# Bounding the decays of a chunked scan on ScalarE, by a relu and an exponential with biases, in place of a subtract-and-min on VectorE

## The chip, the cores and the metric

The kernel runs on one core of a Trainium2 chip. The time of a kernel is the device time of one execution in microseconds (us); lower is better. A profiled execution also leaves a trace, whose span is a little shorter than the execution's time.

## What is computed

The reference is one layer of a hybrid block over 256 tokens with 256 context tokens: a projection, two mixers (S5, a diagonal state space model, and SSD, a chunked scan), a merge, and a mixture of 32 experts. The change lies in SSD, where every head needs, within each chunk of 128 positions, the matrix of decays from position s to position l, times the step dt of position s:

```
def decay_matrix(a_cum):
    ...
    diff = a_cum[..., :, None] - a_cum[..., None, :]
    return jnp.where(mask, jnp.exp(jnp.where(mask, diff, 0.0)), 0.0)
...
    a_cum = jnp.moveaxis(jnp.cumsum(dtc * a.reshape(SSD_GROUPS, SSD_HPG), axis=2), 2, -1)
    cb = jnp.einsum('bclgn,bcsgn->bcgls', cc, bc)
    lmat = decay_matrix(a_cum) * dt_t[..., None, :]
    y_diag = jnp.einsum('bcgls,bcgrls,bcsgrp->bclgrp', cb, lmat, x)
    y_off = jnp.einsum('bclgn,bcgrpn,bcgrl->bclgrp', cc, prev, jnp.exp(a_cum))
```

There are 8 groups of 4 heads, two directions, and two chunks of the 256 tokens: 8 x 2 = 16 sets of 4 x 2 = 8 blocks of 128 x 128.

## The kernel before, in words

The program has three parts in time: some 50 us of preparation, the mixers (50 to 690 us of the span), and then the merge, the router and the experts, which stream 402 MB of weights from memory.

The mixers are written as 14 streams (generators), among them `gemm` (the projection, in blocks of 4 x 128 rows), `conv`, `gates_z`, `prep`, `ssd`, `decays`, and the S5 streams `turned`, `vgen`, `states`, `tables` and `outputs`. A planner (class Plan) takes from them, step by step, the step that could start first by its own cost estimates, and writes the instructions in that order. Each engine (PE, DVE = VectorE, ACT = ScalarE, POOL, and SP, which only starts DMAs) then works through its own list in order. The planner calls all instructions through one helper, so that they all carry line 1442; they are told apart by their tiles.

For each block of `gemm`, SP loads 128 x 512 weights `w`, ACT rounds them to `h` (CAST h<-w), DVE or POOL subtracts to get the rest, again `h` (TENSOR_TENSOR h<-w,h), and PE multiplies both parts into a bank `mm`. At most LOOK = 2 blocks are cut ahead of the one that PE multiplies. Two `mm` banks alternate: a column's bank becomes free when `conv` has read it (one ACT and four DVE instructions for `cv`), when ACT has copied it out (`us`, `zt`), or, for the gate columns at the end, when ACT has taken the sigmoid.

Before the mixers `ssd_dt` makes the cumulative sums `a_cum`: as rows in memory (`acd`), and as columns `acs`, one number per partition, chunk and head. `lnd` is ln(dt), again as columns. Of `acs` ln(dt) is taken off at once (line 441).

`decays` makes set n = 2 g + d_: SP loads four rows of `acd`, each copied to all 128 partitions, as `rt` (one buffer); DVE makes `et` = min(rt - acs, lnd) in 8 instructions of 128 x 128, one for each head and chunk, since acs and lnd are per-partition scalars (lines 922 to 927); ACT takes the exponential of `et` in one instruction of 128 x 1024 and of `rt` in another; POOL multiplies `rt` by C. So et = exp(min(a_l - a_s + ln dt_s, ln dt_s)): where l comes before s the min bounds it, and the mask is multiplied in later. `ssd` then multiplies `et` by the masked C B products `xl` on DVE, and PE multiplies `et` and `rt` into the bank `yps`. When PE has read set n - 1 (mark "used"), `rt` is loaded for set n. The group's output goes on through DVE (`mb`), ACT (`zt`), PE (`aux`), ACT (`rs`) and DVE (`dg`, `ybT`).

Of the kernel before, what the change touches and what calls it, by code (L numbers as in the profile page):

```python
# [13 lines left out]
AF = mybir.ActivationFunctionType  # L14
ALU = mybir.AluOpType
# [4 lines left out]
P = 128  # L20
# [26 lines left out]
def bcast(ap, axis, n):  # L47
    a = ap.unsqueeze(axis)
    shape = list(a.shape)
    shape[axis] = n  # L50
    return a.to_broadcast(shape)


def build(tc, I, out):
    nc = tc.nc
    dve, act, pe, pool, sp = nc.vector, nc.scalar, nc.tensor, nc.gpsimd, nc.sync
# [44 lines left out]
    def aux_ps(name="aux"):  # L101
        return ps.tile([P, 512], F32, tag="aux", name=name, bufs=2)
# [243 lines left out]
    def mm3(out, a, b, first, last):  # L346

        pe.matmul(out, a[0], b[0], start=first, stop=False)
        pe.matmul(out, a[0], b[1], start=False, stop=False)  # L349
        pe.matmul(out, a[1], b[0], start=False, stop=last)  # L350
# [24 lines left out]
    def ux(n):  # L375
        return lambda k: (uh[k // 4][:, k % 4, 0:n], ul[k // 4][:, k % 4, 0:n])
# [8 lines left out]
    def ssd_dt():  # L385
        act.activation(arow, arow, AF.Exp)
        wdh = H.tile([P, KD, 64], F32R, tag="h", name="wdh")
        act.copy(wdh, wdt)
        wdl = H.tile([P, KD, 64], F32R, tag="h", name="wdl")
        dve.tensor_tensor(wdl, wdt, wdh.bitcast(F32), op=ALU.subtract)  # L390
        pd = aux_ps()
        for k in range(KD):
            mm3(pd[0:64], (wdh[:, k], wdl[:, k]), ux(512)(k), k == 0, k == KD - 1)
        dtr = F.tile([64, 512], F32, tag="Ut", name="dtr")
        act.copy(dtr, pd[0:64])
        pt = aux_ps()
        for t in range(4):
            pe.transpose(pt[:, t * 64:(t + 1) * 64], dtr[:, t * P:(t + 1) * P], ident[0:64, 0:64])
        n = [-1]
        dtt = F.tile([P, 4, 4, 64], F32, tag="et", name="dtt", bufs=2)  # L400
        dtt = [dtt[:, i] for i in range(4)] + [F.tile([P, 4, 64], F32, tag="xtok", name="dtq", bufs=BUFS["xtok"])]

        def tt():
            n[0] += 1
            return dtt[n[0]]

        x, e, s_, s2, q = tt(), tt(), tt(), tt(), tt()
        dve.tensor_tensor(x, pt[:, 0:256].rearrange("p (t c) -> p t c", t=4), bcast(dtb, 1, 4), op=ALU.add)
        act.activation(e, x, AF.Abs)
        act.activation(e, e, AF.Exp, scale=-1.0)  # L410

        dve.tensor_scalar(s_, e, 2.0, None, op0=ALU.add)
        dve.reciprocal(s_, s_)
        dve.tensor_mul(s_, s_, e)
        dve.tensor_mul(s2, s_, s_)
        dve.tensor_scalar(q, s2, 1.0 / 15, None, op0=ALU.mult)
        for c_ in (13, 11, 9, 7, 5, 3):
            dve.scalar_tensor_tensor(q, q, 1.0 / c_, s2, op0=ALU.add, op1=ALU.mult)
        dve.scalar_tensor_tensor(q, q, 1.0, s_, op0=ALU.add, op1=ALU.mult)
        dve.tensor_scalar(x, x, 0.0, None, op0=ALU.max)  # L420
        dt = F.tile([P, 4, 64], F32, tag="dg", name="dt")
        dve.scalar_tensor_tensor(dt, q, 2.0, x, op0=ALU.mult, op1=ALU.add)
        dtA = F.tile([P, 4, 64], F32, tag="Cn", name="dtA")
        dve.scalar_tensor_tensor(dtA, dt, -1.0, bcast(arow, 1, 4), op0=ALU.mult, op1=ALU.mult)

        pr = aux_ps()
        pc = aux_ps()
        for c_ in range(2):
            for d_, tr in ((0, triU), (1, triL)):
                cols = slice(32 * d_, 32 * d_ + 32)  # L430
                pe.matmul(pr[cols, c_ * P:(c_ + 1) * P], dtA[:, c_, cols], tr, start=True, stop=True)
                pe.matmul(pc[:, c_ * 64 + 32 * d_:c_ * 64 + 32 * d_ + 32], tr, dtA[:, c_, cols], start=True, stop=True)
        arows = F.tile([64, 256], F32, tag="us", name="arows")
        act.copy(arows, pr[0:64, 0:256])
        acd = dram.tile([64, 256], F32, name="acd")
        act.dma_start(acd, arows)

        lnd = F.tile([P, 2, 64], F32, name="lnd")
        act.activation(lnd, dt[:, 0:2], AF.Ln)
        acs = F.tile([P, 2, 64], F32, name="acs")  # L440
        dve.tensor_tensor(acs, pc[:, 0:128].rearrange("p (c h) -> p c h", c=2), lnd, op=ALU.subtract)

        pw = aux_ps()
        f_, b_ = slice(0, 32), slice(32, 64)
        terms = [
            [(triLs, 2, f_), (ones, 3, f_)], [(triLs, 3, f_)],
            [(triUs, 2, b_)], [(triUs, 3, b_), (ones, 2, b_)],
            [(triLs, 0, f_)], [(triUs, 1, b_)],
            [(ones, 0, f_)], [(ones, 1, b_)],
        ]  # L450
        for i, tl in enumerate(terms):
            for j, (m_, t_, cl) in enumerate(tl):
                pe.matmul(pw[:, 32 * i:32 * i + 32], m_, dtA[:, t_, cl], start=(j == 0), stop=(j == len(tl) - 1))
        wend = F.tile([P, 8, 32], F32, name="wend")
        act.activation(wend.rearrange("p a b -> p (a b)"), pw[:, 0:256], AF.Exp)
        for i, tk, cl in ((0, 2, f_), (1, 3, f_), (2, 2, b_), (3, 3, b_), (4, 0, f_), (5, 1, b_)):
            dve.tensor_mul(wend[:, i, :], wend[:, i, :], dt[:, tk, cl])
        dsm.update(lnd=lnd, acs=acs, wend=wend, acd=acd)
# [6 lines left out]
    def mixers():  # L465
        plan = Plan(nc)
        pe, dve, act, pool, sp = plan.pe, plan.dve, plan.act, plan.pool, plan.sp
        tile_, mark, slot = plan.tile, plan.mark, plan.slot
        EP, Bb, r8, root = s5["EP"], s5["Bb"], s5["r8"], s5["root"]
        lnd, wend, acs, acd = dsm["lnd"], dsm["wend"], dsm["acs"], dsm["acd"]  # L470
# [442 lines left out]
        def decays():  # L913

            for n in range(2 * NG):
                g, d_ = n // 2, n % 2
                plan.at("decay", n / (2 * NG))
                yield ("sp", slot("rt", 1)) + ((("used", n - 1),) if n else ())
                rt = tile_(F, [P, 4, 256], F32, "rt")
                sp.dma_start(rt, acd[32 * d_ + 4 * g:32 * d_ + 4 * g + 4, :].partition_broadcast(P))  # L920
                et = tile_(F, [P, 4, 256], F32, "et", 2)
                for h in range(4):
                    yield "dve", rt
                    for c_ in range(2):
                        hh = 32 * d_ + 4 * g + h
                        dve.tensor_scalar(et[:, h, c_ * P:(c_ + 1) * P], rt[:, h, c_ * P:(c_ + 1) * P],
                                          acs[:, c_, hh:hh + 1], lnd[:, c_, hh:hh + 1], op0=ALU.subtract, op1=ALU.min)
                yield "act", et, AF.Exp
                act.activation(et, et, AF.Exp)
                act.activation(rt, rt, AF.Exp)  # L930
                yield "pool", rt, ("cv", g, 3)
                pool.tensor_tensor(rt, rt, bcast(cv[g, 3][:, 0], 1, 4), op=ALU.mult)
                dec[n] = rt, et
                mark(("dec", n))
# [143 lines left out]
        plan.add(prep(), "prep")  # L1078
        plan.add(ssd(), "out")
        plan.add(decays(), "decay")  # L1080
        plan.add(turned(), "other")
        plan.add(vgen(), "vgen")
# [5 lines left out]
        return ys[0]  # L1088

    ssd_dt()  # L1090
    for q4 in range(4):
        s5_inputs(q4)
# [174 lines left out]
    for t in range(2):  # L1267
# [15 lines left out]
                                 op0=ALU.add, op1=ALU.mult))  # L1283
# [47 lines left out]
class Plan:  # L1331
# [23 lines left out]
    def slot(self, tag, bufs):  # L1355

        of = self.slots.get(tag, [])
        return self.used.get(of[-bufs], 0.0) if len(of) >= bufs else 0.0

    def mark(self, name):  # L1360
        self.ready[name] = self.last
# [585 lines left out]
```

## Time and profile before

| | |
|---|---|
| median of 3 runs | 1853.15 us (1849.97 to 1854.26) |
| the profiled execution | 1846.35 us, span 1844.2 us |
| mixers | about 50 to 690 us of the span |
| busy over the span | PE 86%, DVE 49%, ACT 27%, POOL 16% |

Busy time is the time in which an engine works on an instruction; a wait is the idle time before an instruction, put down to what ended it. All shares below are of one profiled execution. A row's mean can exceed its busy time over its count, where instructions of one kind overlap.

### The profile page before, as it was taken

What the parts mean: (1) busy time and instruction counts of PE and PEld (TensorE: products, weight loads), DVE (VectorE), ACT (ScalarE), POOL (GpSimd) and SP (SyncE); (2) the same over time, 40 slices, a digit from 0 to 9 for tenths busy, and PEclk for the clock granted to TensorE, in tenths of its full rate; (3) what the DMA queues carried; (4) which work ended last, traced back from release to release, by engine and by line L of the source; (5) the groups of instructions that cost most, each with busy time, mean ns of one, the idle gap of its engine ahead of it and who ended that gap; (6) DMA issues with size and microseconds to landing.
All of it is one profiled execution on the core that took longest, in us unless ns stands there. A gap on an engine that the chain in (4) does not pass through costs nothing. (4 is left out here: it accounts for less than half of the span.)

```text
span 1844.2 us, 27968 instructions
## 1 busy us (share of the span) xinstructions
PE 1589.1 (86%) x11118; PEld 935.1 (51%) x11118; DVE 904.5 (49%) x1671; ACT 506.8 (27%) x893; POOL 290.0 (16%) x297
## 2 busy tenths in 40 slices
PE   6798888976988799897998888898888889988987
PEld 3576666764766698783533232333333444333443
DVE  7668899888898546664222222242222223212233
ACT  5333453552435565342111111111111111111111
POOL 5133445435331330100000000000000000000000
PEclk8899898987997999998999999999999999988998
DMA  8677554444542357784999999999998999999984
GB/s 309 181 236 237 178 144 136 119 121 110 148 127 64 114 155 264 235 281 161 417 418 417 417 418 417 413 418 417 418 410 350 418 417 418 418 417 419 418 349 174
DMA packets 141415, 539.36 MB, mean 292 GB/s; under 512 B 31736, under 2 KB 44952, under 8 KB 91920
## 3 DMA queue, kind: packets, MB, share of 16 engines
q1 hardware_dynamic: 136032, 526.95, 75.7%
q10 hardware_dynamic: 4608, 7.95, 1.3%
q8 instruction: 143, 2.34, 0.5%
q0 software_dynamic: 560, 1.52, 0.3%
q14 instruction: 72, 0.59, 0.1%
HBM read 529.60 MB, written 6.77 MB: 291 GB/s over the span
## 5 line engine op out<-in xcount | busy, mean ns | idle before, releaser
L1519 PE MATMUL p_gu<-mw,xe 128*64 128x512 f32 x2048 | 474.8, 601 | 45.2 <-DMA mw<-in_mu 28.4
L1442 PE MATMUL mm<-uh,h 128*128 128x256 f32 (+1 forms) x1152 | 323.6, 361 | 45.2 <-DVE cv L1442 29.9
L1519 PEld LDWEIGHTS p_gu<-mw,xe 128*64 128x64 f32 x2048 | 174.2, 137 | 335.7 <-issue 176.8
L1442 PEld LDWEIGHTS mm<-uh,h 128*128 128x128 f32 x1152 | 209.6, 201 | 85.4 <-issue 42.3
L1629 PE MATMUL p_y<-mw,aT 128*64 128x512 f32 x1024 | 243.4, 627 | 3.4 <-issue 3.4
L1442 PE MATMUL mm<-ul,h 128*128 128x256 f32 (+1 forms) x576 | 202.5, 352 | 0.0
L1442 POOL TENSOR_TENSOR h<-w,h 128x512 fp32r<-128x512 f32 x99 | 150.3, 1522 | 279.3 <-ACT h L1442 213.6
L1637 DVE SCALAR_TENSOR_TENSOR yw<-p_y,gs,xq 64x512 f32<-64x512 f32 x64 | 48.0, 750 | 287.3 <-PE p_y L1629 286.2
L1629 PEld LDWEIGHTS p_y<-mw,aT 128*64 128x64 f32 x1024 | 75.3, 144 | 147.4 <-issue 144.0
L1442 ACT CAST h<-w 128x512 fp32r<-128x512 f32 x144 | 88.1, 618 | 168.7 <-PE mm L1442 121.2
L1442 PEld LDWEIGHTS mm<-ul,h 128*128 128x128 f32 x576 | 116.0, 201 | 13.5 <-issue 3.1
L1533 DVE TENSOR_SCALAR au<-p_gu 128x512 f32<-128x512 f32 x32 | 22.1, 692 | 198.7 <-PE p_gu L1519 198.7
L1639 ACT CAST yh<-yw 64x512 fp32r<-64x512 f32 x64 | 39.4, 616 | 285.4 <-DVE yw L1637 285.4
L1527 DVE TENSOR_SCALAR ag<-p_gu 128x512 f32<-128x512 f32 (+1 forms) x34 | 23.0, 676 | 169.8 <-PE p_gu L1519 169.8
L1442 DVE SCALAR_TENSOR_TENSOR cv<-mm,cw,cv 128x508 f32<-128x508 f32 (+3 forms) x128 | 85.6, 673 | 11.0 <-ACT cv L1442 10.6
L359 DVE TENSOR_TENSOR low<-w,hi 128x512 fp32r<-128x512 f32 x80 | 59.6, 751 | 41.6 <-ACT hi L357 40.3
L1528 ACT ACTIVATE as<-ag 128x512 f32<-128x512 f32 (+1 forms) x34 | 21.0, 617 | 210.5 <-DVE ag L1527 210.5
L1442 ACT ACT_TABLE_LOAD x55 | 70.6, 1283 | 29.9 <-DVE cv L1442 29.1
L357 ACT CAST hi<-w 128x512 fp32r<-128x512 f32 x80 | 49.4, 620 | 70.3 <-PE mm L349 24.8
L1613 PE MATMUL p_t<-ident,au 128*128 128x128 f32 x128 | 30.5, 325 | 39.7 <-PEq L1730 25.2
L1442 DVE TENSOR_SCALAR et<-rt,acs,lnd 128x128 f32<-128x128 f32 x128 | 45.9, 413 | 23.6 <-DMA rt<-acd 23.4
L1442 DVE TENSOR_TENSOR h<-w,h 128x512 fp32r<-128x512 f32 x45 | 39.2, 872 | 31.8 <-ACT h L1442 31.8
(452 smaller groups left out, 2335.2 us busy)
## 6 DMA issues: line engine op xcount, KB each, us to landing
mw<-in_mg SPq DMA_DIRECT2D x128, 1024.0 KB
mw<-in_mu SPq DMA_DIRECT2D x128, 1024.0 KB
mw<-in_md SPq DMA_DIRECT2D x128, 1024.0 KB
w<-in_wg SPq DMA_DIRECT2D x96, 256.0 KB
ada<-in_ada SPq DMA_DIRECT2D x32, 256.0 KB
Toe<-in_ada SPq DMA_DIRECT2D x16, 512.0 KB
vT<-Ed SPq DMA_DIRECT2D x16, 512.0 KB
l8a<-in_ada SPq DMA_DIRECT2D x16, 512.0 KB
```

The source lines that it names most:

```text
L357: act.copy(hi, w)
L359: lo.tensor_tensor(low, w, hi.bitcast(F32), op=ALU.subtract)
L1442: return fn(*args, **kw)
L1519: mm = pe.matmul(dst[c * q:c * q + c, 0:n], lhs(k), w[:, o:o + n], start=(i == 2 and k == 0), stop=(k == KD - 1))
L1527: dve.tensor_scalar(g_, pg, 7.0, None, op0=ALU.min)
L1528: sg = act.activation(s_, g_, AF.Sigmoid, scale=1.702)
L1533: dve.tensor_scalar(u_, pu, -7.0, 7.0, op0=ALU.max, op1=ALU.min)
L1613: pe.transpose(pa[:, q * P:(q + 1) * P], u_[:, q * P:(q + 1) * P], ident)
L1629: self.done = pe.matmul(py[64 * q:64 * q + 64], aT[:, k % 4, k // 4], wts[e, 2, c // load.unit][:, c % load.unit:c % load.unit + 512], sta ...
L1637: dve.scalar_tensor_tensor(w[rows], self.py[rows], self.gs[rows, nh, j:j + 1], gf[rows, 512 * nh:512 * nh + 512], op0=ALU.mult, op1=ALU.mult)
L1639: act.copy(self.hi[rows, nh], w[rows])
```

## The change

The columns `acs` no longer have ln(dt) taken off. `et` is made on ACT in two passes over the 8 blocks: relu(acs - rt), with scale -1 and acs as a bias pointer, and then exp(lnd - that), with scale -1 and lnd as a bias pointer. Since -relu(a_s - a_l) = min(a_l - a_s, 0), that is the same number. DVE's 8 instructions are gone, and so is ACT's one exponential over all of `et`.

```
-        dve.tensor_tensor(acs, pc[:, 0:128].rearrange("p (c h) -> p c h", c=2), lnd, op=ALU.subtract)
+        dve.tensor_copy(acs, pc[:, 0:128].rearrange("p (c h) -> p c h", c=2))
...
-                for h in range(4):
-                    yield "dve", rt
-                    for c_ in range(2):
-                        hh = 32 * d_ + 4 * g + h
-                        dve.tensor_scalar(et[:, h, c_ * P:(c_ + 1) * P], rt[:, h, c_ * P:(c_ + 1) * P],
-                                          acs[:, c_, hh:hh + 1], lnd[:, c_, hh:hh + 1], op0=ALU.subtract, op1=ALU.min)
+                for f, src, by in ((AF.Relu, rt, acs), (AF.Exp, et, lnd)):
+                    for h in range(4):
+                        yield "act", src, f
+                        for c_ in range(2):
+                            hh = 32 * d_ + 4 * g + h
+                            cl = slice(c_ * P, c_ * P + P)
+                            act.activation(et[:, h, cl], src[:, h, cl], f, scale=-1.0, bias=by[:, c_, hh:hh + 1])
                 yield "act", et, AF.Exp
-                act.activation(et, et, AF.Exp)
                 act.activation(rt, rt, AF.Exp)
```

The planner orders everything anew. Over the whole program ACT's list goes from 16 instructions `et<-et` of 128x1024 to 128 `et<-rt,acs` and 128 `et<-et,lnd` of 128x128, and from 55 loads of a function table at line 1442 to 53; of the 144 subtractions `h<-w,h` DVE gets 49 instead of 45 and POOL 95 instead of 99. Other counts stay.

ACT's list at the first set, before (`us` are copies out of an `mm` bank, `cv` a convolution's tile):

```order
L455 ACTIVATE wend<-aux 128x256
L1442 COPY us<-mm 128x8x8 x4
L1442 COPY us<-mm 128x8x32
L1442 CAST h<-w 128x512 x2
L1442 COPY us<-mm 128x8x8 x4
L1442 COPY us<-mm 128x8x32
L1442 ACTIVATE et<-et 128x1024
L1442 ACTIVATE rt<-rt 128x1024
L1442 CAST h<-w 128x512
```

and now:

```order
L1442 COPY us<-mm 128x8x32
L1442 CAST h<-w 128x512
L1442 ACTIVATE et<-rt,acs 128x128 x8
L1442 ACTIVATE et<-et,lnd 128x128 x6
L1442 COPY us<-mm 128x8x8 x4
L1442 COPY us<-mm 128x8x32
L1442 ACTIVATE et<-et,lnd 128x128 x2
L1442 ACTIVATE rt<-rt 128x1024
L1442 CAST h<-w 128x512
```

One of the two casts that stood ahead of the set now stands behind all of it.

DVE's list in the middle of the mixers, around a set that stood there (`Wt` and `vtw` belong to S5's `outputs`):

```order
 L1442 TENSOR_TENSOR vtw<-EP,Ct 128x512
 L1442 SCALAR_TENSOR_TENSOR Wt<-Wt,vtw 128x512
-L1442 TENSOR_SCALAR et<-rt,acs,lnd 128x128 x8
-L1442 TENSOR_TENSOR vtw<-EP,Ct 128x512
-L1442 TENSOR_TENSOR h<-w,h 128x512
-L1442 TENSOR_TENSOR et<-et,xl 128x4x128 x2
```

The set's eight instructions leave the list; what followed them is placed anew.

ACT's list at the last set, before:

```order
L1442 CAST h<-w 128x512 x3
L1442 ACT_TABLE_LOAD
L1442 ACTIVATE et<-et 128x1024
L1442 ACTIVATE rt<-rt 128x1024
L1442 ACT_TABLE_LOAD
L1442 ACTIVATE xl<-mm 128x256 x2
```

and now:

```order
L1442 CAST h<-w 128x512
L1442 ACTIVATE et<-rt,acs 128x128 x8
L1442 ACT_TABLE_LOAD
L1442 ACTIVATE et<-et,lnd 128x128 x8
L1442 ACTIVATE rt<-rt 128x1024
L1442 CAST h<-w 128x512
L1442 ACT_TABLE_LOAD
```

Sixteen instructions stand there with no cast among them, and the table load stands between the two passes. Counted through ACT's new list, 5 of the 16 sets have no cast between the first relu and the exponential of `rt`; the other 11 have one or more.

## Rows read from the trace of the kernel before

**Rows 1.** Busy time of each engine in four stretches: the mixers' start, middle, end, gate columns.
```profile
50.00:150.00 100.00, 89.70 (x827) 67.41 (x826) 68.94 (x143) 34.88 (x70) 22.39 (x15) 0.94 0.77 224
150.00:600.00 450.00, 373.02 (x3411) 293.04 (x3410) 395.62 (x733) 196.21 (x313) 193.08 (x192) 0.88 0.47 134
600.00:652.00 52.00, 39.48 (x377) 33.22 (x375) 27.57 (x50) 30.15 (x42) 15.97 (x9) 0.90 0.35 101
652.00:690.00 38.00, 37.96 (x344) 37.89 (x345) 16.28 (x26) 24.78 (x46) 14.51 (x12) 1.00 0.59 178
```
**Rows 2.** Waits of PE, 150 to 600 us: total us, times, longest.
```profile
PE mm L1442 <- DVE cv L1442: 29.9, 8, 11.8
PE yps L1442 <- DVE et L1442: 9.6, 5, 6.2
PE mm L1442 <- POOL h L1442: 9.0, 3, 4.3
...
PE s L1442 <- DVE V L1442: 4.4, 5, 1.6
PE aux L1442 <- DVE xw L1442: 4.3, 1, 4.3
PE y L1442 <- DVE l4a L1442: 3.4, 2, 2.0
...
PE aux L1442 <- DVE dg L1442: 2.5, 3, 1.7
```
**Rows 3.** Waits of DVE, 150 to 600 us.
```profile
DVE et L1442 <- DMA rt<-acd: 9.6, 4, 5.5
DVE cv L1442 <- ACT cv L1442: 8.0, 2, 4.1
DVE strip L1442 <- ACT strip L1442: 6.6, 2, 5.5
DVE h L1442 <- ACT h L1442: 6.0, 3, 4.8
```
**Rows 4.** Groups by shape: busy us, mean ns | idle before; the first from 150 to 600 us.
```profile
L1442 DVE TENSOR_SCALAR et<-rt,acs,lnd 128x128 f32<-128x128 f32 x96 | 36.3, 427 | 9.8 <-DMA rt<-acd 9.6
...
L1442 DVE TENSOR_SCALAR et<-rt,acs,lnd 128x128 f32<-128x128 f32 x128 | 45.9, 413 | 23.6 <-DMA rt<-acd 23.4
L1442 DVE TENSOR_TENSOR h<-w,h 128x512 fp32r<-128x512 f32 x45 | 39.2, 872 | 31.8 <-ACT h L1442 31.8
```
**Rows 5.** ACT's groups by shape, the whole mixers.
```profile
L1442 ACT ACTIVATE et<-et 128x1024 f32<-128x1024 f32 x16 | 17.0, 1060 | 21.4 <-DVE et L1442 21.3
...
L1442 ACT COPY us<-mm 128x64 f32<-128x64 f32 x32 | 4.4, 222 | 4.7 <-PE mm L1442 2.3 <-DMA U<-us 2.3
L1442 ACT COPY strip<-w 128x128 f32<-128x128 f32 x16 | 4.2, 265 | 7.0 <-PE w L1442 6.9
...
L1132 ACT ACTIVATE sg<-mm,glub 128x256 f32<-128x256 f32 x4 | 1.9, 470 | 0.8 <-DVE yal L1135 0.8
...
L1442 ACT ACTIVATE mb<-mm 128x256 f32<-128x256 f32 x4 | 1.5, 384 | 0.1
...
L439 ACT ACTIVATE lnd<-dt 128x128 f32<-128x128 f32 x1 | 0.3, 310 | 0.0
```
**Rows 6.** Timeline at the first set: start us, us, engine, instruction [idle before].
```profile
82.64 0.62 ACT L1442 CAST h<-w 128x512 fp32r<-128x512 f32 x1 [2.18 <-PE mm L1442]
...
84.87 2.15 DVE L1442 TENSOR_SCALAR et<-rt,acs,lnd 128x128 f32<-128x128 f32 x8 [3.69 <-DMA rt<-acd]
...
81.04 0.63 PE L1442 MATMUL mm<-uh,h 128*128 128x512 f32 x2
81.74 0.63 PE L1442 MATMUL mm<-uh,h 128*128 128x512 f32 x2
```
**Rows 7.** Timeline at the last two sets.
```profile
620.21 2.14 DVE L1442 TENSOR_SCALAR et<-rt,acs,lnd 128x128 f32<-128x128 f32 x8 [4.81 <-DMA rt<-acd]
...
636.76 2.14 DVE L1442 TENSOR_SCALAR et<-rt,acs,lnd 128x128 f32<-128x128 f32 x8 [5.34 <-DMA rt<-acd]
...
634.84 1.28 ACT L1442 ACT_TABLE_LOAD   x1
639.90 1.04 ACT L1442 ACTIVATE rt<-rt 128x1024 f32<-128x1024 f32 x1
...
643.58 1.98 PE L1442 MATMUL yps<-rt,bt 128*64 128x128 f32 x16 [0.66 <-POOL rt L1442]
```

## The prediction

> **What bounds the kernel now.** I read the stretches first. In the middle of the mixers, from 150 to 600 us, VectorE is busy 395.6 of 450 us (88%), PE 373.0 (83%), ACT 196.2 (44%) [rows 1]. At the start (50 to 150 us) PE leads with 90%; from 600 to 652 us no engine is above 76%, so a chain of single steps sets the time there; from 652 us on PE is never idle. The reader should see that VectorE is the fullest engine only in the middle, and that ACT has more than half of that stretch free.
>
> The waits come second, since a full engine need not be the one others wait for. PE is idle 450 - 373 = 77 us in the middle. Of that, VectorE ends 29.9 us (a bank `mm` that the convolution has not yet read), 9.6 (`et`), 4.4, 4.3, 3.4 and 2.5, together 54.1 us or 70%; a subtraction on POOL ends 9.0 [rows 2]. VectorE in its turn is idle 54 us, and waits 9.6 us for `rt` to land and 8.0 + 6.6 + 6.0 = 20.6 us for ACT [rows 3]. So in the middle VectorE is the engine that is late, and PE can gain at most about 54 us from a faster VectorE. What follows the mixers starts when they end and is untouched by the edit; a microsecond saved in the mixers is taken as a microsecond of the whole.
>
> **What the change takes off VectorE.** The 128 instructions of `et` take 45.9 us in all, and VectorE stands idle 23.4 us before them because `rt` has not landed [rows 4]. In the middle, where VectorE is short, there are 96 of them with 36.3 us, and 9.6 us of these waits [rows 3, 4]. Four subtractions `h` move from POOL to VectorE; at 872 ns each [rows 4] they add 3.5 us, and I put all of them in the middle. VectorE's list there gets shorter by 36.3 + 9.6 - 3.5 = 42.4 us. The copy that replaces the subtraction for `acs` is one instruction for one and costs nothing.
>
> **What it adds on ACT.** The trace has no ACT instruction of 128x128 from SBUF with a bias pointer, so I build it. Without a pointer the logarithm `lnd` of that very shape takes 310 ns. A sigmoid of 128x256 with one bias pointer (`sg`) takes 470 ns against 384 without (`mb`): 86 for the pointer, so 396 ns. Instructions in a row overlap: the small copies `us` last 222 ns each, but 32 of them fill 4.4 us, 137 each, so 85 are covered [rows 5]. That leaves 311 ns, and 16 for a set are 5.0 us. Over all sets 256 x 0.311 = 79.6 us, less the 17.0 us of the 16 wide exponentials [rows 5] and two table loads of 1.28 [rows 7]: ACT gets 60 us more. From below, the copy `strip` of 128x128 without a pointer takes 265 ns [rows 5], 180 with the overlap, which makes it 26 us more; from above, no overlap at all makes it 82. I keep 311, since the shape is the same and the pointer is seen by itself.
>
> **What of it lies on the path.** In the middle ACT gets 12 of the 16 sets, 45 us, and goes from 196 to 241 of 450 us, 54%: it is not full. But its list is in order and others wait for it. I let VectorE's 20.6 us of waits for ACT grow with ACT's busy time, by 45/196: 4.7 us (2 to 6 by the bounds). Of VectorE's 42.4 us I count the 70% of PE's idle time that VectorE ends today: 29.7 us.
>
> This can be set against two places of the skill. The Trainium skill, page "ScalarE: Activation LUTs", section "Rules for kernel authors", says to use VectorE and not ScalarE for relu and min. By its rule the engine time would go up, by 60 on ACT against 42.4 off VectorE, and the change would lose some 18 us, about 1871. The page "Perfetto Trace Analysis", section "Optimizing Scalar/DVE Operations", says that moving work to Scalar may pay where DVE is saturated; by that the middle gains. The stretch with VectorE at 88% and ACT at 44% [rows 1] is nearer to the second.
>
> At both ends the change costs. **The start:** the first `rt` lands at 84.87 us, and VectorE waited for it [rows 6]. Now ACT waits there, and the cast that ran at 82.64 [rows 6] stands behind the whole set: 84.87 + 5.0, five small copies of 0.137 and 1.04 for the exponential of `rt` [rows 5, 7] give 91.6, 9.0 us late. PE holds two cut blocks; three multiplications take 0.70 us (81.04 to 81.74 [rows 6]), twelve 2.8, two blocks 5.6. It runs dry for about 3.4 us. **The end:** the last two sets stand in the chain, with VectorE idle until `rt` lands, at 620.21 and 636.76 us, and PE multiplying only after POOL's product with `rt` [rows 7]. From landing to the exponential of `rt` it took 639.90 - 636.76 = 3.1 us, now 5.0, and at the last set the table load of 1.28, which lay in idle time at 634.84 [rows 7], stands between the passes: 1.9 + 1.9 + 1.3 = 5.1 us later.
>
> **The sum:** -29.7 + 4.7 + 3.4 + 5.1 = -16.5 us. The profiled execution took 1846.35 us, 1844.2 of them in the span, and would take about 1830. It lies 6.8 us below the median of the runs, 1853.15, and under their lowest, so I take the difference from the median: **1836 us, 0.9% faster.** With 50% or 100% of the 42.4 us in place of 70%, the sum runs from -8 to -29: the likeliest case's own range is 1824 to 1845.
>
> **Rivals.**
> *All of VectorE's time comes back, and more.* For it: stretches with VectorE working without a pause while PE waits are the largest entries of PE's waits, up to 11.8 us at once [rows 2], and PE's clock in the middle stands at 0.88 of full speed against 1.00 in the gate columns, where PE never waits [rows 1]; a PE that waits less may run faster too. Then the whole 42.4 us count, and ends and ACT cost nothing: 1811 us. Against it: PE is itself busy 83% there.
> *ACT holds up the casts: slower.* The place is PE's wait for `h`. A set with no cast in it holds ACT for 5.0 + 1.28 + 1.04 = 7.3 us. PE has 5.6 us in hand, of which the cast (0.62 [rows 6]) and a subtraction (0.87) use 1.5, so PE stands for 7.3 - 4.1 = 3.2 us each time. Five sets of the new order have no cast in them; five such stops cost 16 us and use up the gain. It decides from the sixth on: eight make 1836 + 26 = 1862. For it: ACT now waits for `rt` too, where VectorE did, up to 5.5 us at once [rows 3], with casts behind it. Against it: PE waits only 9.0 us for POOL's `h` in the middle today [rows 2], and in 11 sets casts stand between the new instructions. The skill's rule against relu on ScalarE ends on the same side.
> *No change.* The order is planned anew, and the time that VectorE gets is eaten by just such stops, or PE finds its next wait: 1853 us. For it: PE and VectorE are only five points apart [rows 1].
>
> **Chances.** Forecast 0.47, all of it back 0.18, no change 0.14, slower 0.21. A measurement of this kernel can tell about 0.2% (3.7 us) from no change, so faster has 0.65, the same 0.14, slower 0.21. The range reaches from a little under the large gain to the eight stops: 1806 to 1862 us. The bounds of the ACT price move the ends by 2 us and the two chains by some 6, within it.
>
> **What the new profile would show.** VectorE's group `et<-rt` is gone, and its busy time from 150 to 600 us falls by some 30 us; if not, the first step is wrong. ACT's new groups take about 311 ns of busy time each, 80 us in all; at 180 or 400 the price is wrong. PE's waits for VectorE's `cv` fall well below 29.9 us; if they stay, VectorE was not what was late. PE's waits for `h` (POOL's and VectorE's together) stay under 25 us; above 40 the slower rival holds. The gate columns begin some 17 us earlier than before, and all that follows keeps its length. The prediction is wrong in sign if the new order makes ACT's list the one that PE waits for, and wrong in size if PE's clock or the planner's new placing of S5 steps moves the end of the mixers by more than the sum.

## The result and the profile after

The changed kernel takes 1861.45 us (median of 5 runs, 1858.18 to 1863.92), the kernel before in the same session 1853.63. The ratio is 1.0054, with a 95% interval of 1.0030 to 1.0079: 0.5% slower, inside the predicted range and on the other side of zero. The profiled execution has a span of 1856.1 us.

The stretches of the changed kernel, columns as in [rows 1] (start and end, length, busy us of PE, of PE's weight loads, of DVE, ACT and POOL, each with its number of instructions, then PE's granted clock as a share of the full one, the DMA engines' busy share, and GB/s):

```profile
50.00:150.00 100.00, 84.39 (x790) 64.13 (x792) 69.49 (x122) 43.40 (x101) 27.13 (x19) 0.90 0.73 218
150.00:600.00 450.00, 371.20 (x3298) 293.92 (x3295) 370.04 (x636) 237.58 (x488) 176.57 (x187) 0.90 0.47 136
600.00:652.00 52.00, 44.43 (x519) 36.68 (x518) 24.80 (x44) 33.83 (x72) 14.37 (x9) 0.84 0.33 100
652.00:690.00 38.00, 35.72 (x328) 34.36 (x328) 13.27 (x22) 22.77 (x42) 13.18 (x11) 0.96 0.57 170
```

In the middle VectorE fell from 395.6 to 370.0 us and ACT rose from 196.2 to 237.6, both as foretold. PE did not move: 373.0 before, 371.2 now, idle 77 then and 79 now. VectorE's own idle time grew instead, from 54 to 80 us. What it waits for there, and then what PE waits for (both 150 to 600 us; total us, times, longest):

```profile
DVE mb L1442 <- PE yps L1442: 12.0, 3, 10.0
DVE vtv L1442 <- DMA V<-Bd: 10.9, 5, 3.6
DVE xw L1442 <- PE aux L1442: 9.0, 8, 2.8
DVE rot L1442 <- PE s L1442: 8.4, 3, 6.2
```
```profile
PE mm L1442 <- DVE cv L1442: 23.7, 6, 7.6
PE yps L1442 <- DVE et L1442: 11.2, 7, 3.0
PE yps L1442 <- POOL rt L1442: 8.4, 2, 8.2
```

The first of PE's lines answers to 29.9 us and the second to 9.6 in [rows 2]. VectorE had 25 us more, and PE still waited 23.7 us for VectorE to free a bank `mm`: VectorE's list now waits for PE and for transfers at other places.

ACT's new groups (busy us, mean ns | idle before):

```profile
L1442 ACT ACTIVATE et<-et,lnd 128x128 f32<-128x128 f32 x128 | 40.9, 391 | 0.2
L1442 ACT ACTIVATE et<-rt,acs 128x128 f32<-128x128 f32 x128 | 40.0, 392 | 9.2 <-DMA rt<-acd 9.2
```

80.9 us over 256 instructions are 316 ns each; 311 and 79.6 us had been worked out. The wait for `rt` to land moved with the work, from VectorE [rows 4] to ACT, but it is 9.2 us in place of 23.4.

ACT's timeline at the first set and at the last (start us, us):

```profile
83.68 2.46 ACT L1442 ACTIVATE et<-rt,acs 128x128 f32<-128x128 f32 x8 [2.39 <-DMA rt<-acd]
86.04 1.85 ACT L1442 ACTIVATE et<-et,lnd 128x128 f32<-128x128 f32 x6
87.80 0.78 ACT L1442 COPY us<-mm 128x64 f32<-128x64 f32 x5
88.47 0.70 ACT L1442 ACTIVATE et<-et,lnd 128x128 f32<-128x128 f32 x2
89.06 1.06 ACT L1442 ACTIVATE rt<-rt 128x1024 f32<-128x1024 f32 x1
90.01 0.62 ACT L1442 CAST h<-w 128x512 fp32r<-128x512 f32 x1
...
632.70 2.45 ACT L1442 ACTIVATE et<-rt,acs 128x128 f32<-128x128 f32 x8
635.17 1.28 ACT L1442 ACT_TABLE_LOAD   x1
636.46 2.44 ACT L1442 ACTIVATE et<-et,lnd 128x128 f32<-128x128 f32 x8
638.81 1.04 ACT L1442 ACTIVATE rt<-rt 128x1024 f32<-128x1024 f32 x1
```

From landing to the end of the exponential of `rt` the first set takes 90.12 - 83.68 = 6.4 us (6.7 worked out); the last reaches that exponential 6.1 us after its first relu (6.3 worked out), with the table load between the passes. These prices hold; what they do to the end is another matter. The last set's exponential of `rt` ends at 639.85 us, where it ended at 640.94 before [rows 7], so the last decays are not late. Of the 16 sets, 11 end it earlier than before and five later, by 0.3 to 15.5 us. The S5 outputs are late: ACT's last copy of `strip` from `w`, and PE's first instruction behind the mixers, each in the kernel before and then in the changed one:

```profile
608.67 0.25 ACT L1442 COPY strip<-w 128x112 f32<-128x112 f32 x1 [1.44 <-PE w L1442]
684.58 1.86 PE L1185 MATMUL aux<-rw,shc 128*128 128x32 f32 x16
```
```profile
631.45 0.25 ACT L1442 COPY strip<-w 128x112 f32<-128x112 f32 x1 [1.10 <-PE w L1442]
687.71 1.87 PE L1185 MATMUL aux<-rw,shc 128*128 128x32 f32 x16
```

The last `strip` from `w` comes 22.8 us later, the last from `y` 10.4, the end of the mixers 3.1. The spans differ by 11.9; the other 8.8 arise behind the mixers, where no line differs, and stay unexplained. In the twenty traces of this case that last part takes from 1156 to 1172 us (1160 before, 1168 in the changed kernel), so one execution of each cannot tie the 8.8 us to the edit. (The medians are 7.8 apart.)

### The profile page after: what moved, and what is told of

Same layout as the page of the kernel before. It is cut to its first block, busy times and chain, and to the rows that moved or that the text cites. A ratio compares the mean times of both kernels' runs of the same rounds, so it can differ in the third digit from the quotient of the medians.

```text
span 1856.1 us, 28063 instructions
## 1 busy us (share of the span) xinstructions
PE 1589.0 (86%) x11118; PEld 934.3 (50%) x11118; DVE 874.5 (47%) x1547; ACT 559.9 (30%) x1131; POOL 274.3 (15%) x293
## 5 line engine op out<-in xcount | busy, mean ns | idle before, releaser
L1442 PE MATMUL mm<-uh,h 128*128 128x256 f32 (+1 forms) x1152 | 322.0, 359 | 38.0 <-DVE cv L1442 23.9
L1519 PEld LDWEIGHTS p_gu<-mw,xe 128*64 128x64 f32 x2048 | 170.0, 137 | 341.9 <-issue 176.3
L1442 POOL TENSOR_TENSOR h<-w,h 128x512 fp32r<-128x512 f32 x95 | 135.2, 1428 | 323.7 <-ACT h L1442 258.9
L1442 PEld LDWEIGHTS mm<-ul,h 128*128 128x128 f32 x576 | 115.6, 201 | 11.9 <-issue 1.4
L1442 DVE SCALAR_TENSOR_TENSOR cv<-mm,cw,cv 128x508 f32<-128x508 f32 (+3 forms) x128 | 85.8, 674 | 16.5 <-ACT cv L1442 15.5
L1613 PE MATMUL p_t<-ident,au 128*128 128x128 f32 x128 | 29.9, 319 | 39.2 <-PEq L1730 25.6
L1614 ACT COPY aT<-p_t 128x256 f32<-128x256 f32 x64 | 23.8, 373 | 110.7 <-PE p_t L1613 110.6
```

Of the source, the lines that this page charges most:

```text
L1442: return fn(*args, **kw)
L1519: mm = pe.matmul(dst[c * q:c * q + c, 0:n], lhs(k), w[:, o:o + n], start=(i == 2 and k == 0), stop=(k == KD - 1))
L1613: pe.transpose(pa[:, q * P:(q + 1) * P], u_[:, q * P:(q + 1) * P], ident)
L1614: act.copy(aT[:, 2 * h:2 * h + 2].rearrange("p a b s -> p (a b s)"), pa[:, 256 * h:256 * h + 256])
```

## The experiments

Two causes are mixed in the result: where the work stands, and the order that the planner makes of it. My theory after the result was that ACT's price is larger than the sum had it; the rival, that the new order is the loss. Ratios below are to the kernel before, each with its 95% interval; us are worked out with 1850 us for 1.

**Lists held.** The planner's calls are numbered as they are made. Behind the plan, every engine's instructions in the mixers are tied one behind the other in a list given beforehand, by dependencies that only set the order. The list is that of the built kernel before ("old lists") or of the changed one ("new lists"). The steps that the list was planned with are charged, but not issued, and what is tried is put in their place. Two kernels below keep this only in part: VectorE's eight instructions in the new lists and POOL's subtraction in the old ones are not tied themselves and stand where the program issues them. The kernel before and the changed kernel are compared as they were planned, and no run has them with the ties.

```
             made = fn(*args, **kw)
+            plan.made.append([made.ins] if made is not None else [])
...
         plan.run()
+        stand(tc, plan.made)
```

*The work on ACT, and on neither engine, in the old lists.* For the first, the 16 relus and exponentials stand where the wide exponential stood; for the second:

```
-                act.activation(et, et, AF.Exp)
+                plan.made[-1].append(nc.scalar.activation(et, rt, AF.Exp).ins)
```

with VectorE's eight instructions gone. 

> The edit in the old order: every engine's list in the mixers is held to that of the kernel before; VectorE's 128 instructions of et are taken out of it, and the relus and exponentials stand on ACT where the wide exponential stood. If the new order gave the gain away, this is faster than before by 10 to 25 us (1829 to 1844 us). If VectorE was not what the mixers wait for, it is within 6 us of before (1848 to 1860). If ACT's longer stay holds up the casts, it is slower than before by 8 us or more (1862 and up), and PE's waits for h rise above 25 us.

> The old order again, VectorE's et left out and nothing put in its place: ACT's wide exponential reads rt, so the min and the difference are left out of the computation. It is the most that taking the work off VectorE can give in this order. If VectorE is late, 15 to 40 us faster than before (1814 to 1839); if it is not, within 8 us of before. The difference to the run with the work on ACT is the price of ACT's 60 us: under 10 us if ACT's list has room, 20 or more if it holds up others.

Measured: 1.0101 (1.0085 to 1.0117) with the work on ACT, 0.9908 (0.9892 to 0.9925) without it. So leaving the work out is worth 17 us here, and putting it on ACT costs 36. The 17 us hold two things that no run separates: VectorE's free time, and the step that is gone between the landing of `rt` and the exponential. PE's wait for `cv`, 29.9 us before, did not fall with the work gone (50 to 700 us):

```profile
PE mm L1446 <- DVE cv L1446: 33.4, 9, 13.6
```

*How much of the 36 us is ACT's longer list, and how much that `et` and `rt` come later.* The work is left out as before, and ACT gets instructions behind the exponential of `rt` that nobody waits for:

```
+                for f, src, by in ((AF.Relu, ident[:, 0:56], acs), (AF.Exp, spare, lnd)):
+                    for h in range(3):
+                        for c_ in range(2):
+                            hh = 32 * d_ + 4 * g + h
+                            made = nc.scalar.activation(spare, src, f, scale=-1.0, bias=by[:, c_, hh:hh + 1])
+                            plan.made[-1].append(made.ins)
```

with `range(5)` and `h % 4` in the first kernel. 

> Every engine's list is that of the kernel before; `et` is the plain wide exponential of `rt` (the difference and the bound by ln(dt) are left out), and ACT gets 20 further instructions behind the exponential of `rt` in each set: 10 relus and 10 exponentials of 128x56 with a bias pointer into a tile that nobody reads, about 5 us a set by an estimate from the 311 ns of the 128x128 ones. So ACT is as busy as in old_order_act, but nothing waits for those instructions. If ACT's price (old_order_act 1.0101 of the kernel before, old_order_none 0.9908) is that its list is full, this one is near 1.008 to 1.010, 1867 to 1872 us. If the price is that `et` and `rt` themselves come later for VectorE's and POOL's products, it is near 0.993, some 1840 us. Half of each gives 1.000.

> As old_order_busy, with 12 further instructions a set in place of 20 (6 relus and 6 exponentials of 128x56 into a tile that nobody reads). There they took 341 ns each and did not overlap, so the 20 filled 109 us and not the 80 intended; 12 fill 65 us, which is what old_order_act has more than old_order_none (80.9 less 17.0 = 64 us). The difference and the bound are left out of `et` again. If ACT's price is that its list is longer, whoever waits, this stands near old_order_act, 1.006 to 1.011, 1861 to 1870 us. If a good part is that `et` and `rt` themselves come late, it stands at 0.998 to 1.003.

Measured: 1.0201 (1.0176 to 1.0226) with 20, 1.0025 (1.0004 to 1.0047) with 12. ACT's groups in the kernel with 12:

```profile
L939 ACT ACTIVATE spare<-spare,lnd 128x56 f32<-128x56 f32 x96 | 32.8, 342 | 3.1
L939 ACT ACTIVATE spare<-ident,acs 128x56 f32<-128x56 f32 x96 | 32.6, 340 | 2.6
```

That is 65 us of ACT's time, as much as the work itself adds, and it costs 1.0025 - 0.9908 = 1.2%, 22 us. The other 1.0101 - 1.0025 = 0.8%, 14 us, is put down to the later `et` and `rt`, and the waits show where. VectorE for `et` and POOL for `rt`, 50 to 700 us, in the kernel with 12 idle instructions, then with the work on ACT:

```profile
DVE et L1454 <- ACT et L933: 5.7, 3, 3.5
...
POOL rt L1454 <- ACT rt L1454: 55.6, 11, 18.8
```
```profile
DVE et L1452 <- ACT et L936: 31.3, 8, 10.1
...
POOL rt L1452 <- ACT rt L1452: 106.3, 13, 22.7
```

VectorE's product with `xl` waits 31.3 us in place of 5.7, and everything behind it in VectorE's list waits too; PE waits 21.8 us for that product in place of 10.2. The price of a longer list also grows with its length: 65 us cost 22, 109 us cost 54.

*The same in the new lists.* Neither engine, and VectorE:

```
-                            act.activation(et[:, h, cl], src[:, h, cl], f, scale=-1.0, bias=by[:, c_, hh:hh + 1])
+                            said["act"].activation(et[:, h, cl], src[:, h, cl], f, scale=-1.0, bias=by[:, c_, hh:hh + 1])
+                            if f == AF.Relu:
+                                nc.vector.tensor_scalar(et[:, h, cl], rt[:, h, cl], acs[:, c_, hh:hh + 1], lnd[:, c_, hh:hh + 1],
+                                                        op0=ALU.subtract, op1=ALU.min)
```

(`said` charges and does not issue.) 

> Every engine's list is that of the changed kernel, but `et` is the plain wide exponential of `rt` (the difference and the bound are left out on both engines). If the changed kernel's order is as good as the old one when the work is on neither engine, this stands at 0.991 of the kernel before, 1837 us, and the work on ACT costs some 25 us in the new order too. If the new order is better suited, since it was planned with VectorE free, it stands at 0.985 or under. If the new order is by itself the loss, it stands at 1.000, and the work on ACT costs only some 10 us there.

> Every engine's list is that of the changed kernel, with the eight subtract-and-min instructions of a set back on VectorE near the place where the relus stood, and the one wide exponential on ACT. If the order alone makes the changed kernel slow, this stands at 1.005 or above. If the order is neutral, it stands at 1.000 plus or minus 0.3%. If the order is planned for a VectorE without that work, VectorE is late again and this stands near 1.010.

Measured: 1.0032 (1.0012 to 1.0052) and 1.0195 (1.0177 to 1.0213). Put together:

| `et` is made on | old lists | new lists |
|---|---|---|
| neither (left out) | 0.9908 | 1.0032 |
| VectorE | 1 | 1.0195 |
| ACT | 1.0101 | 1.0054 |

In the new lists the edit gains 1.4%, in the old ones it costs 1.0%. Each list does best with the placing that it was planned for; in the other cell the work stands at places that no planner chose, so part of the 1.0% and of the 1.4% can be those places. The new lists cost 1.2% even with the work gone. PE's first wait in the new lists, with the work on neither engine and then on VectorE:

```profile
PE mm L1448 <- DVE cv L1448: 31.3, 8, 7.8
```
```profile
PE mm L1451 <- DVE cv L1451: 41.5, 12, 8.9
```

With the work back on VectorE PE waits 41.5 us for a bank `mm`, against 23.9 in the changed kernel over the same stretch (50 to 710 us): that is in kind the gain that the prediction had looked for. But with the work on neither engine it is 31.3, so this wait by itself does not measure the gain.

**Other places for the work, in the old lists.** `et` in two wide instructions on VectorE, and with the subtraction on POOL:

```
+                h4 = slice(32 * d_ + 4 * g, 32 * d_ + 4 * g + 4)
+                made = nc.vector.tensor_tensor(et.rearrange("p h (c l) -> p c h l", c=2), rt.rearrange("p h (c l) -> p c h l", c=2),
+                                               bcast(acs[:, :, h4], 3, P), op=ALU.subtract)
+                plan.made[-1].append(made.ins)
+                made = nc.vector.tensor_scalar(et, et, 80.0, None, op0=ALU.min)
+                plan.made[-1].append(made.ins)
```

> The lists of the kernel before; all of the computation is there, and ACT has nothing more than before. VectorE makes `et` in two wide instructions in place of eight: a subtraction of 128x1024 with acs spread over the positions, and a minimum with a constant of 80 (acs has ln(dt) taken off, so the kept part needs no bound; the masked part only has to stay finite). By the rows of 128x512 products (0.68 us each) and of the 128x1024 scaling `xall` (0.75 us) that is 1.36 + 0.75 = 2.1 us a set for 2.87, 12 us less over the whole. At the worth that old_order_none gave to VectorE's 46 us (17 us), this gains 4 to 5 us: 0.997 to 0.998, about 1845. If VectorE's work is worth nothing by itself, 1.000.

> As old_order_wide, with the wide subtraction on POOL, whose product of the same shape takes 2.56 us; VectorE keeps the minimum (0.75 us a set, 12 us in all, 34 less than before), POOL gets 41 us more. If POOL is as free as its 43% busy time in the middle says, VectorE's relief is worth 34/46 of 17 us = 12 us: 0.993 to 0.994, 1837. If the longer way from landing to the exponential and POOL's list (its subtractions `h` queue behind) cost as ACT's list did, 0.5 us for each us, then 1.004 or above.

Measured: 1.0021 (1.0003 to 1.0039) and 1.0100 (1.0076 to 1.0124): neither gains. The groups of the first and of the second:

```profile
L930 DVE TENSOR_TENSOR et<-rt,acs 128x1024 f32<-128x1024 f32 x16 | 20.8, 1302 | 13.6 <-DMA rt<-acd 13.5
...
L933 DVE TENSOR_SCALAR et<-et 128x1024 f32<-128x1024 f32 x16 | 13.0, 813 | 0.5
```
```profile
L930 POOL TENSOR_TENSOR et<-rt,acs 128x1024 f32<-128x1024 f32 x16 | 31.6, 1972 | 32.3 <-DMA rt<-acd 29.1 <-PE mm L1452 3.1
...
L933 DVE TENSOR_SCALAR et<-et 128x1024 f32<-128x1024 f32 x16 | 16.7, 1045 | 35.3 <-POOL et L930 35.2
```

VectorE took 12 us less for `et` (33.8 for 45.9) and nothing came of it. But its busy time over the mixers fell only from 504.3 to 500.9 us, since others of its instructions took longer, and the step between landing and exponential is still there; so this says little about what a free VectorE is worth. On POOL the way gets longer: VectorE now stands 35.2 us waiting for POOL, with its list behind it.

**The order alone.** One number of the planner, NEAR (how many ns later than the first possible step a step may start and still be chosen), moves the order, and with it where a few subtractions `h` run (VectorE gets 43 to 46 of the 144 in the kernel before, 46 to 49 in the changed one) and how many table loads there are:

```
-NEAR = 260
+NEAR = 270
```

> The kernel before, with one constant of the planner (the 260 ns within which steps count as ready together) set to 270: the same instructions in another order. If the order by itself is worth little, within 4 us of before; if it is worth as much as the edit, 6 us or more off to either side.

> The changed kernel with the same constant at 270. If the order by itself is worth little, within 4 us of the changed kernel's 1861; if it is worth as much as the edit, 6 us or more off to either side.

> The kernel before with one number of the planner, NEAR, at 250 in place of 260: the same instructions in another order. With 270 it stood at 1.0087. If the order as such moves this kernel by up to 1%, this one is off by some tenths of a per cent, most likely upward, 1.002 to 1.010, since 260 is the lowest of what was seen so far; if 270 was an accident, it stands within 0.2%.

> The changed kernel with the planner's NEAR at 250: the same instructions, and few places of the order differ from 260. If the order is what moves these kernels by a per cent, whatever the edit, this differs from the 1.0054 of the changed kernel by some tenths, and may come out under 1.000; the kernel before with 250 stood at 1.0069. If the changed kernel loses by its work and not by its order, it stays within 1.004 to 1.007.

> The kernel before with NEAR at 280. 250 gave 1.0069 and 270 1.0087: if 260 is a lucky order, 1.003 to 1.010 here too; if orders scatter evenly around that of 260, 0.995 to 1.002.

> The changed kernel with NEAR at 280; 250, 260 and 270 gave 1.0058, 1.0054 and 1.0090 of the kernel before. At 250 and 270 the two kernels stood within 0.1% of each other. If the edit is worth nothing over orders, this stands within 0.4% of before_near280 on either side; if it costs half a per cent by itself, it stands 0.4% or more above it.

| NEAR | kernel before | changed kernel |
|---|---|---|
| 250 | 1.0069 (1.0049 to 1.0090) | 1.0058 (1.0035 to 1.0080) |
| 260 | 1 | 1.0054 (1.0030 to 1.0079) |
| 270 | 1.0087 (1.0069 to 1.0106) | 1.0090 (1.0067 to 1.0112) |
| 280 | 1.0086 (1.0058 to 1.0114) | 1.0065 (1.0043 to 1.0086) |

The kernel before stands lowest at 260 by 0.7%. At the other three the two kernels differ by -0.1, 0.0 and -0.2%, less than the intervals can tell.

**The planner free, with the work left out or with traced charges.** First `et` is the plain exponential of `rt`, planned anew. Then ACT's 128-wide instructions with a bias are charged what they take, with NEAR at 260 and at 270; and in the kernel before VectorE's:

```
-            return 60 + 0.85 * n + switch
+            return (210 if n == P and "bias" in kw else 60) + 0.85 * n + switch
...
-        return 63 + (0.52 if fast else 1.05) * n
+        return (292 if op == "tensor_scalar" and n == P else 63) + (0.52 if fast else 1.05) * n
```

> The kernel before with `et` as the plain wide exponential of `rt` (difference and bound left out), and the planner free to order it, as it is for the kernels before and after. In the old lists this work left out gave 0.9908, in the changed kernel's lists 1.0032. If a planner's order is a draw that moves the time by up to a per cent, this lands between 0.990 and 1.003 with nothing to say where, most likely near 0.997, 1845 us. If the planner makes good use of a freed VectorE whenever ACT is not burdened, it is at 0.990 or below.

> The changed kernel with one cost of the planner changed: an ACT instruction over 128 elements with a bias is charged 319 ns in place of 169, which is what the 256 of them took in the trace (80.9 us in all, 316 each). If the changed kernel loses because the planner believes its sets to be done 2.4 us earlier than they are, this gains most of a per cent: 0.995 to 1.000. If the price is that ACT's list is long and the order a draw, it stays between 1.002 and 1.010.

> after_true_cost with NEAR at 270, where the changed kernel stands at 1.0090 of the kernel before. If the charge is what spoiled the changed kernel's order, this is lower than that by about as much as at 260 (0.8%): 0.999 to 1.003. If the gain at 260 was a lucky draw, it stands within 0.3% of 1.0090.

> The kernel before with the planner charging a VectorE instruction of two scalars over 128 elements 359 ns (45.9 us over 128 of them) in place of 130, so that both kernels can be compared with the trace's durations in the plan. If knowing the price always helps, this is below 1.000, near 0.996, and the edit gains nothing over it. If the old order is already a good draw, a new one lands above it, 1.002 to 1.009 as with 250, 270 and 280.

Measured: planned_none 0.9826 (0.9803 to 0.9849), after_true_cost 0.9975 (0.9960 to 0.9991), after_true_cost270 1.0072 (1.0048 to 1.0097), before_true_cost 1.0155 (1.0130 to 1.0180). The middle stretch of planned_none:

```profile
150.00:600.00 450.00, 382.46 (x3582) 303.44 (x3582) 389.92 (x661) 207.32 (x330) 191.54 (x197) 0.93 0.49 139
```

PE is busy 9 us more there than in [rows 1]: with the work gone and the order free, VectorE's time does reach PE, 32 us by the medians. In the traced execution it is 23.6 us, 22 of them in the mixers. after_true_cost is the one complete kernel here that beats both, at 1844.87 us; but the same charge gains 0.2% at NEAR 270, inside the intervals, and the corrected charge in the kernel before loses 1.6%. So wrong charges are not shown to be the cause; 0.9975 is one good order more.

**How PE takes it.** PE from 50 us to the end of its last block of the projection, in the kernel before and with the work on neither engine in the old lists (columns as above):

```profile
50.00:684.62 634.62, 534.78 (x4909) 426.19 (x4907) 504.34 (x942) 282.56 (x461) 245.95 (x227) 0.90 0.51 148
```
```profile
50.00:666.47 616.47, 520.92 (x4926) 416.49 (x4926) 465.56 (x816) 283.12 (x461) 241.16 (x228) 0.93 0.53 153
```

The same reading for seven kernels, one traced execution each:

| kernel | PE busy, us | PE idle, us | granted clock |
|---|---|---|---|
| before | 534.8 | 99.8 | 0.90 |
| changed | 533.5 | 104.3 | 0.90 |
| neither, old lists | 520.9 | 95.6 | 0.93 |
| ACT, old lists | 539.1 | 119.0 | 0.89 |
| VectorE, new lists | 543.2 | 121.8 | 0.88 |
| neither, new lists | 529.0 | 104.3 | 0.91 |
| neither, planner free | 526.3 | 86.2 | 0.93 |

PE has the same matrix multiplications to do in all seven. Of the 18 us by which the mixers get shorter in the old lists with the work gone, only 4 are waits of PE; in the other 14 PE does the same work in less time, at a higher granted clock. In the new lists some 17 of 32 us are waits, and with the planner free 14 of 22. Why the clock is granted higher there is not shown.

## Why the prediction was wrong

**The failed steps.** Two prices of the sum were mis-sized, and it lacked a term. ACT's price was put at "4.7 + 3.4 + 5.1" = 13.2 us; with the order held as before it is 36 us, 22 for the longer list and 14 for the later `et` and `rt`. VectorE's relief was put at 29.7 us; with the order held it is 17. So the edit loses 19 us before anything is reordered, where the sum gained 16.5. For the middle the sum had let VectorE's waits grow with ACT's busy time; it missed that one wide instruction became 16 in a row, with a product waiting behind them. The term that it lacked is the order: the planner made a new one, which is 1.2% worse than the old with the work on neither engine, and yet gives back 9 us of the loss; that it does so because it was planned for this placing is likely, but not shown.

**The gain of 29.7 us.** Measured, it is 17 us in the old lists, 30 (1.0195 - 1.0032) in the new and 32 with the planner free. The size is met in two orders of three, but the sum had counted waits of PE alone, and of the gain in the mixers only 4, 17 and 14 us are waits in the traced executions; the rest is PE at a higher granted clock, which only the rival "all of VectorE's time comes back" had named. That 70% of 42.4 us came near is luck.

**In the old lists** the books are -17 + 22 + 14 = +19 us, and the new order takes 9 of them back: +10. In the new lists they read +36 (that order with the work on VectorE) - 30 + 4 = +10. Both ways are measured, and the parts are not the same, so no single number is the worth of this edit. By the second way ACT's price is 4 us, which the intervals cannot tell from nothing, and the order is the whole loss; what failed either way is that the sum priced the edit in one order and got another. Over four NEARs it is +0.5, -0.1, 0.0 and -0.2%: nothing that can be told, and a loss at 260, where the kernel before has its best order of the four.

**The signs that were named.** VectorE's busy time fell by 25.6 us where some 30 had been told, and ACT's groups took 316 ns: right. PE's waits for `cv` were to fall well below 29.9 and stand at 23.7, at 33.4 in the old lists with the work gone, and in the new lists at 31.3 with the work gone and 41.5 with it on VectorE: whether freeing VectorE shortens that wait depends on the order, and in the old one it does not. PE's waits for `h` (VectorE's and POOL's) stayed under 25 us: they are 3.4 us from 50 to 690 us, where they were 12.6. The mixers were to end 17 us earlier and ended 3.1 later.

**The ends.** The 3.4 and 5.1 us stood on chains that were priced rightly (6.4 and 6.1 us), and did not show. At the first set PE did not run dry: it is busy for the whole 10.1 us from 84.9 to 95.0 us. The last set's exponential ends 1.1 us before its old time, since the new order makes the last decays earlier and the S5 outputs later.

**The rivals.** The slower one gave 1862 us by stops of PE at `h`; the time came true and the mechanism did not. "No change" named the new order as what would eat the gain, and that is the nearest to what was found; it wanted a chance well above 0.14, for the order alone moves the unchanged kernel by up to 1.6%. "All of VectorE's time comes back", 1811 us, is what planned_none comes near to (1817.27), without ACT's load, and the faster PE that it named is seen there: a granted clock of 0.93 in the middle for 0.88. The Trainium skill, page "ScalarE: Activation LUTs", section "Rules for kernel authors", would keep relu off ScalarE; 1871 us had been worked out by that. In the old lists the measured time agrees, 1.0101 and 1869.52 us, but not by its terms (60 against 42.4 us there, 36 against 17 measured); in the new lists it doesn't, since there the edit gains.

**What stays open.** Why the kernel before is that good at 260, and which of the displaced steps makes the new lists dearer with the work gone: the later S5 outputs are seen, their price is not. Why PE's granted clock differs between these kernels, and how much of each price is the clock's. And the 8.8 us behind the mixers.

## What to carry to other kernels

Where a planner decides the order, hold each engine's list fixed and price the edit in it, and see how far a change of one harmless number moves the time, before believing in half a per cent of either sign. Moving work to an engine with much idle time is not free: when its list is in order, count the new instructions as delay for everything queued behind, and for the consumer of their last result, most of all when one wide instruction becomes many. A kernel's present order can be a low draw (here 260 is the lowest of four by 0.7%), and an edit that reorders it then starts with that as a debt.

## What was not expected of the hardware

A VectorE instruction that reads two tiles from SBUF can stand still while POOL works. Its products of 128x512 in the kernel before (ns least/median/most), and one of them with its neighbours:

```profile
L1442 DVE TENSOR_TENSOR et<-et,xl x32: 676/684/2672, 124.2 to 640.6; 128x512 f32<-128x512 f32 x32
```
```profile
581.70 2.67 DVE L1442 TENSOR_TENSOR et<-et,xl 128x512 f32<-128x512 f32 x1
...
584.44 0.68 DVE L1442 TENSOR_TENSOR et<-et,xl 128x512 f32<-128x512 f32 x1
```
```profile
581.46 2.37 POOL L1442 TENSOR_TENSOR rt<-rt,cv 128x1024 f32<-128x1024 f32 x1 [17.93 <-ACT rt L1442]
584.41 1.84 POOL L1442 TENSOR_TENSOR h<-w,h 128x512 fp32r<-128x512 f32 x1 [0.58 <-ACT h L1442]
```

POOL's product runs from 581.46 to 583.83; VectorE's, started 0.24 us later, ends at 584.37, some 0.54 us after POOL's. All eight of these products that take over 1.1 us end 0.55 us after a POOL instruction that had started before them. The twin 2.7 us later takes 0.68, though a POOL instruction overlaps it; there it is POOL's that is long, 1.84 us against a median of 1.30. The mean of the 32 is 972 ns in the kernel before and 776 in the changed one, which is 6 us of VectorE's time that comes from the order and not from the edit. The Trainium skill, page "GPSIMD Engine Reference", section "Key points", says that the two engines share their way into SBUF for VectorE's instructions with two SBUF inputs; the trace agrees. A busy time read in one order is therefore not a price in another.
